# V turned by VectorE through HBM, and small TensorE tasks grouped, in the first stage of a hybrid decoder trunk

## The chip, the cores and the metric

The kernel runs on one core of a Trainium2 chip. The metric is device time in microseconds (us), from start to end of one execution. A core has five engines that run their own instruction lists side by side: TensorE (PE, matrix products, with its weight loads as PEld), VectorE (DVE), ScalarE (ACT), GpSimd (POOL) and SyncE (SP), which here issues nearly all transfers between HBM and the core's own memory (SBUF). TensorE writes its results into PSUM, from where DVE and ACT read them.

## The reference, cut to what matters

One layer: a norm, one input projection (2048 columns to 8 attention heads and 4 retention heads), both kinds of head, an output projection with a residual add, and a gated MLP with a short convolution. 16 meta tokens stand ahead of 256 tokens; the projections run over T = 272 tokens.

```python
proj = u @ w_in[l]
aq, ak, av, rq, rk, rv, rg = jnp.split(proj, SPLITS, axis=-1)
# diff_attention, per head: two softmaxes of 64 columns each, V of 128 columns
s = jnp.where(mask[None, None, None], s + bias[None, :, None], NEG_INF)
p = jax.nn.softmax(s, axis=-1)
a = (p[:, :, 0] - lam * p[:, :, 1]).astype(v.dtype)
return jnp.einsum('bhqk,bkhe->bqhe', a, v)
# retention, per head: scores times a decay table, V of 256 columns
s = jnp.einsum('bnihd,bnjhd->bnhij', q, k) * decay_in.astype(dt)[None, None]
intra = jnp.einsum('bnhij,bnjhe->bnihe', s, v)
...
ya = rmsnorm(ya, attn_subln[l]) * (1.0 - lam_init)
yr = rmsnorm(yr, ret_norm[l]) * jax.nn.silu(rg.reshape(B, L, R_HEADS, R_V_DIM))
y = jnp.concatenate([ya.reshape(B, L, D_A), yr.reshape(B, L, D_R)], axis=-1)
h = h + y @ w_out[l]
u = rmsnorm(h, ffn_norm[l]) * vmask
h = h + conv_glu(u, w_gate[l], w_up[l], conv_w[l], w_down[l])
```

Both kinds of head need V with the keys on the partitions, since the product of weights and values sums over keys. The kernel takes retention over the whole sequence at once, with decay tables in place of the chunks.

## The kernel before, in words

**The large products.** Features lie on the partitions, tokens in columns. A gemm makes one tile of 128 output features by 272 tokens (258, NQ, where the 14 leading ones are not needed) in PSUM, over 16 blocks (k-tiles) of 128 input features. Each block takes three products (L292 to L294): high part of the weight times high part of x, high times low, low times high, which together keep float32's precision. So a gemm is 48 matmuls. The weights of one gemm are one chunk of 1 MB (128 x 2048), loaded by SP (L95) into one of three `raw` buffers; ACT casts a half chunk into the high part `whi` (L107) and DVE subtracts to get the low part `wlo` (L108), three buffers each. Before each half gemm, `ahead` issues loads about two chunks forward and casts three halves forward.

**The first stage** takes the input projection. For each of 8 attention heads there are three gemms (q, k, v), for each of 4 retention heads four (k, q and two halves of v) and two more for its gates; the order of retention's parts is RSEQ: y0, g0, y1, g1, y2, y3, g2, g3. DVE multiplies each result with the norm's factor on its way out of PSUM (L546 for retention's v). Behind it come the output projection (16 gemms, L556 to L578, which also turns its results with DVE and stores them into an HBM scratch, `hd`, L573 and L576), 44 pairs of gate and up gemms, and the down projection.

**The heads' own work** is cut into small tasks, which wait in the list `side`; each gemm takes one task from it after every quarter (`pump`), so that they stand in TensorE's queue between the gemms' matmuls. All small matmuls and transposes are plain float32; a transpose is a matmul with the identity. An attention head has 12 tasks: the bias, three scores (softmax and difference, A), `vtr` (L371), three `atr` (L379), `av` (L391), `ytr` (L406) and two empty ones. `vtr` transposes V's three blocks of keys (100, 86 and 86 keys, KB) and copies them out of PSUM; `atr(i)` transposes the i + 1 blocks of A's row i; `av` makes the values and scales them; `ytr` transposes the head's result. A retention head has 10: three scores, three `vtr`, two `av` (one per half of V), `stats` (two products with ones, `rst`, and a reciprocal root) and `scale`; then two gate tasks. A program's names carry the head's number: `pv2` is the PSUM tile of V's transposes of attention head 2, `py` of the result's, `pa` of A's, `po` the values; `rv`, `rs` and `ro` are retention's V transposes, scores and values.

**The order.** The program is written gemm by gemm, but what each engine's list looks like in the end is set by a scheduler, which plays the program through with modelled durations when the kernel is built (`schedule_with_timeline_sim=True` in `build`) and appends what is ready. PSUM's eight banks bound it: three hold gemm results (`mm`), three are for small tasks (`misc`), two for scores of a head (`sc`, one buffer).

Of the kernel before, what the change touches and what calls it, by code (L numbers as in the profile page):

```python
# [10 lines left out]
F32 = mybir.dt.float32  # L11
# [4 lines left out]
ALU = mybir.AluOpType  # L16
# [3 lines left out]
P = 128  # L20
# [4 lines left out]
T = META + SEQ  # L25
Q0 = META - 2
NQ = T - Q0
QT = NQ // 3
TW = 288
XO = 32 - META  # L30
GO = 30
# [28 lines left out]
def trunk_kernel(ctx, tc, a, out):  # L60
# [91 lines left out]
    def misc(name):  # L152
        return ps1.tile([P, 512], F32, tag="misc", bufs=3, name=name)
# [145 lines left out]
    with ExitStack() as p1:  # L299
# [20 lines left out]

        nop = lambda: None

        def att_tasks(h, q, k, v):
            slope = 2.0 ** (-(h + 1))
# [45 lines left out]

            def vtr():  # L371
                ps = misc(f"pv{h}")
                for j, (b, e) in enumerate(KB):
                    PE.transpose(ps[:e - b, j * P:(j + 1) * P], v[:, b:e], idt)
                V.tensor_copy(out=vt[:KB[0][1], 0], in_=ps[:KB[0][1], :P])
                V.tensor_copy(out=vt[:QT, 1:3].rearrange("p a b -> p (a b)"),
                              in_=ps[:QT, P:3 * P])

            def atr(i):  # L379
                def f():  # L380
                    ps = misc(f"pa{h}_{i}")
                    for j in range(i + 1):
                        b, e = KB[j]
                        PE.transpose(ps[:e - b, j * P:j * P + QT], As[i][:, b:e], idt[:QT, :QT])
                    for j in range(i + 1):
                        b, e = KB[j]
                        (V.tensor_copy if j else S.copy)(
                            out=at[j][:e - b, i - j], in_=ps[:e - b, j * P:j * P + QT])
                return f

# [15 lines left out]
            def ytr():  # L406
                ps = misc(f"py{h}")
                for i in range(3):
# [9 lines left out]
        def ret_tasks(r, k, q, vs):  # L418
            dt_ = ap_.tile([P, 2, NQ], F32, tag="t", name=f"dk_{r}")
# [7 lines left out]

            def scores(j):
                def f():
                    b, e = KB[j]  # L430
                    n = (3 - j) * QT
                    ps = misc(f"rs{r}_{j}")
                    PE.matmul(ps[:e - b, :n], k[:, b:e], q[:, j * QT:], start=True, stop=True)
                    V.tensor_tensor(out=sd[j][:e - b], in0=ps[:e - b, :n], in1=dk[j],
                                    op=ALU.mult)
                return f

            def vtr(j):
                def f():
                    b, e = KB[j]  # L440
                    ps = misc(f"rv{r}_{j}")
                    for c in range(2):
                        PE.transpose(ps[:e - b, c * P:(c + 1) * P], vs[c][:, b:e], idt)
                    S.copy(out=vt[:e - b, j], in_=ps[:e - b, :2 * P])
                return f

            def av(c):
                def f():
                    if c == 0:
                        st["y"] = ps1.tile([P, 2, 512], F32, tag="sc", bufs=1, name=f"ro{r}")  # L450
                    y = st["y"]
                    cs = slice(c * P, (c + 1) * P)
                    for j, (b, e) in enumerate(KB):
                        n = e - b
                        o = y[:, c, j * QT:NQ]
                        PE.matmul(o, vt[:n, j, cs], sd[j][:n], start=(j == 0), stop=(j == 2))  # L456
# [3 lines left out]
                return f  # L460

# [14 lines left out]
            def scale():  # L476
                for c in range(2):
# [23 lines left out]
        for h in range(AH):  # L501
            q = ap_.tile([P, NQ], F32, tag="q", name=f"q{h}")
            k = ap_.tile([P, T], F32, tag="k", name=f"k{h}")
            v = ap_.tile([P, T], F32, tag="v", name=f"v{h}")
            ps = gemm(idx, xhi, xlo, Q0, NQ, 1)
            V.scalar_tensor_tensor(out=q, in0=ps[:, :NQ], scalar=0.125, in1=rq_,
                                   op0=ALU.mult, op1=ALU.mult)
            ps = gemm(idx + 1, xhi, xlo, 0, T, 1)
            V.tensor_tensor(out=k, in0=ps[:, :T], in1=rk_, op=ALU.mult)
            ps = gemm(idx + 2, xhi, xlo, 0, T, 1)  # L510
            V.tensor_tensor(out=v, in0=ps[:, :T], in1=rk_, op=ALU.mult)
            idx += 3
# [12 lines left out]
            side.extend(att_tasks(h, q2, (k2, kl), v))  # L525
        for kind, r in RSEQ:
            if kind == "g":
                for c in range(2):
                    g = ap_.tile([P, NQ], F32, tag=f"g{c}", name=f"rg{r}_{c}")
                    ps = gemm(idx, xhi, xlo, Q0, NQ, 1)  # L530
# [10 lines left out]
            V.tensor_tensor(out=q, in0=ps[:, :NQ], in1=rq_, op=ALU.mult)  # L541
            vs = []
            for c in range(2):
                v = ap_.tile([P, T], F32, tag="e" if c else "v", name=f"rv{r}_{c}")
                ps = gemm(idx + 2 + c, xhi, xlo, 0, T, 1)
                V.tensor_tensor(out=v, in0=ps[:, :T], in1=rk_, op=ALU.mult)  # L546
                vs.append(v)
            idx += 4
            side.extend(ret_tasks(r, k, q, vs))
        pump(len(side))  # L550
# [5 lines left out]
        for j in range(KT):  # L556
            xr = ap_.tile([P, NQ], F32, tag="g0", name=f"xres{j}")
            nc.sync.dma_start(out=xr, in_=a["x"][:, j, Q0:T])
            ps = gemm(idx + j, yhi, ylo, 0, NQ, 1)
            hT = ap_.tile([P, NQ], F32, tag="g1", name=f"hT{j}")  # L560
            V.tensor_tensor(out=hT, in0=ps[:, :NQ], in1=xr, op=ALU.add)
# [249 lines left out]
```

## Time and profile before

| | |
|---|---|
| median of the runs | 1181.98 us (1181.56 to 1183.25) |
| the profiled execution's own time | 1181.89 us |
| its span | 1180.1 us, granted TensorE clock 0.999 |
| TensorE busy | 1168.3 us, 99% of the span |
| first stage, 20 to 350 us | TensorE busy 329.2 of 330.0, DVE 253.8, ACT 177.8, DMA share 0.46 |
| output projection, 350 to 440 us | TensorE busy 89.1 of 90.0, DMA share 0.75 |
| gate and up gemms and what follows, 440 to 900 us | TensorE busy 460.0 of 460.0 |

The span runs from the first to the last instruction that the profiler saw; the execution's time is 1.8 us longer. A group's row shows line, engine, operation, written tile <- read tiles, partitions and shape, how many, then busy time, mean ns of one, and the idle time before them with what ended it. A row of the timeline shows start and duration in us. TensorE's matmuls overlap, so that their durations add up to more than the time they take. In rows for stretches of time the columns are the engines' busy times, the granted clock, the DMA share (mean busy share of 16 DMA engines) and GB/s.

### The profile page before, as it was taken

The page shows a single profiled execution, that of the slowest core. Times are in us where ns is not written, and L with a number is a line of the kernel's source. Part 1 is how long each engine was busy: PE and PEld are TensorE (multiplying, and loading weights), DVE is VectorE, ACT ScalarE, POOL GpSimd, SP SyncE. Part 2 cuts the span into 40 slices and gives each one's busy share as a digit, 9 for nine tenths or more (in the row PEclk, how much of TensorE's full clock was granted, in tenths as well). Part 3 has the DMA queues.
Part 4 walks back from the last instruction along what each step waited for, and adds up shares of the span by engine and source line. Part 5 has one row for each costly group of instructions (what it writes and reads, how often), then busy time and mean ns, then how long its engine had stood idle before and what let it go on. Part 6 is the DMA issues. An engine that isn't in the chain of part 4 may idle for free.

```text
span 1180.1 us, 19961 instructions
## 1 busy us (share of the span) xinstructions
PE 1168.3 (99%) x8087; PEld 1093.1 (93%) x8087; DVE 804.0 (68%) x1450; ACT 564.0 (48%) x887; POOL 2.0 (0%) x7
## 2 busy tenths in 40 slices
PE   9999999999999999999999999999999999999997
PEld 8999999999999999999999999999999888888886
DVE  7898877667677777776667776767767645454544
ACT  7566665544345444444444444444444434343442
POOL 0000000000000000000000000000000000000000
PEclk9999999999999999999999999999999999999999
DMA  8544344444448776555555555555555655555552
GB/s 308 189 154 160 144 144 157 167 166 146 151 156 262 227 226 230 184 192 195 180 179 182 188 195 185 179 180 190 191 190 179 214 207 186 194 198 183 194 194 106
DMA packets 53661, 219.82 MB, mean 186 GB/s; under 512 B 21763, under 2 KB 26091, under 8 KB 28609
## 3 DMA queue, kind: packets, MB, share of 16 engines
q1 hardware_dynamic: 53280, 217.36, 52.7%
q8 instruction: 63, 1.03, 0.3%
q0 software_dynamic: 144, 1.05, 0.2%
q14 instruction: 30, 0.24, 0.1%
q10 hardware_dynamic: 144, 0.14, 0.0%
HBM read 214.34 MB, written 4.19 MB: 185 GB/s over the span
## 4 chain that ended last, share of the span: by engine, by line
PE 97%; DMA 1%; DVE 1%; ACT 0%; issue 0%; SPq 0%; DVEq 0%; ACTq 0%
PE mm L292 17%; PE mm L293 17%; PE mm L294 17%; PE mm L288 14%; PE mm L290 7%; PE o L645 7%; PE o L646 7%; PE o L644 7%; PE po L396 1%; PE ro L456 1%; DMA raw<-in_w_first_dram 1%; PE mm L213 1%; PE mm L211 1%; PE mm L212 1%; PE mm L287 0%; PE sc L346 0%
## 5 line engine op out<-in xcount | busy, mean ns | idle before, releaser
L108 DVE TENSOR_TENSOR wlo<-raw,whi 128x1024 fp32r<-128x1024 f32 x381 | 466.1, 1224 | 245.8 <-ACT whi L107 240.7
L107 ACT CAST whi<-raw 128x1024 fp32r<-128x1024 f32 x381 | 400.3, 1051 | 472.6 <-PE mm L293 245.7
L288 PE MATMUL mm<-g,whi 128*128 128x512 f32 x704 | 249.1, 392 | 0.0
L292 PE MATMUL mm<-x,whi 128*128 128x272 f32 (+1 forms) x688 | 200.2, 291 | 0.0
L293 PE MATMUL mm<-g,whi 128*128 128x258 f32 x704 | 199.8, 284 | 0.0
L292 PE MATMUL mm<-g,whi 128*128 128x258 f32 x704 | 199.4, 283 | 0.0
L293 PE MATMUL mm<-x,whi 128*128 128x272 f32 (+1 forms) x688 | 199.2, 290 | 0.0
L294 PE MATMUL mm<-g,wlo 128*128 128x258 f32 x704 | 198.8, 282 | 0.0
L294 PE MATMUL mm<-x,wlo 128*128 128x272 f32 (+1 forms) x688 | 197.4, 287 | 0.8 <-DVE wlo L108 0.8
L290 PE MATMUL mm<-g,wlo 128*128 128x256 f32 x660 | 185.2, 281 | 0.0
L288 PEld LDWEIGHTS mm<-g,whi 128*128 128x128 f32 x704 | 132.1, 188 | 26.1
L293 PEld LDWEIGHTS mm<-g,whi 128*128 128x128 f32 x704 | 132.4, 188 | 1.9
L294 PEld LDWEIGHTS mm<-g,wlo 128*128 128x128 f32 x704 | 132.9, 189 | 0.0
L292 PEld LDWEIGHTS mm<-g,whi 128*128 128x128 f32 x704 | 132.4, 188 | 0.0
L294 PEld LDWEIGHTS mm<-x,wlo 128*128 128x128 f32 x688 | 129.6, 188 | 1.0 <-DVE wlo L108 1.0
L645 PE MATMUL o<-wlo,fhi 128*128 128x512 f32 x334 | 130.0, 389 | 0.0
L646 PE MATMUL o<-whi,flo 128*128 128x512 f32 x334 | 129.9, 389 | 0.0
L293 PEld LDWEIGHTS mm<-x,whi 128*128 128x128 f32 x688 | 129.7, 189 | 0.1
L292 PEld LDWEIGHTS mm<-x,whi 128*128 128x128 f32 x688 | 129.7, 188 | 0.1
L290 PEld LDWEIGHTS mm<-g,wlo 128*128 128x128 f32 x660 | 124.3, 188 | 0.0
L644 PE MATMUL o<-whi,fhi 128*128 128x512 f32 x334 | 117.0, 389 | 0.0
L644 PEld LDWEIGHTS o<-whi,fhi 128*128 128x128 f32 x334 | 62.7, 188 | 13.0
(245 smaller groups left out, 1376.3 us busy)
## 6 DMA issues: line engine op xcount, KB each, us to landing
raw<-in_w_in_dram SPq DMA_DIRECT2D x44, 1024.0 KB, 4.9
raw<-in_w_gate_dram SPq DMA_DIRECT2D x44, 1024.0 KB, 4.8
raw<-in_w_up_dram SPq DMA_DIRECT2D x44, 1024.0 KB, 4.8
raw<-in_w_down_dram SPq DMA_DIRECT2D x44, 1024.0 KB, 4.8
raw<-in_w_out_dram SPq DMA_DIRECT2D x16, 1024.0 KB, 5.0
raw<-in_w_first_dram SPq DMA_DIRECT2D x6, 512.0 KB, 7.6
xres<-in_x_dram SPq DMA_DIRECT2D x16, 129.0 KB, 4.5
hd<-hb SPq DMA_DIRECT2D x64, 32.0 KB, 3.7
```

What stands on the lines that cost most here:

```text
L107: S.copy(out=hi, in_=src)
L108: V.tensor_tensor(out=lo, in0=src, in1=hi.bitcast(F32), op=ALU.subtract)
L211: PE.matmul(o, wh, xh, start=(k == 0), stop=False)
L212: PE.matmul(o, wh, xl, start=False, stop=False)
L288: PE.matmul(ps[:, :2 * n], wh, xb, start=(k == 0), stop=(k == KT - 1))
L290: PE.matmul(ps[:, :n], wl, xh, start=False, stop=False)
L292: PE.matmul(ps[:, :n], wh, xh, start=(k == 0), stop=False)
L293: PE.matmul(ps[:, :n], wh, xl, start=False, stop=False)
L294: PE.matmul(ps[:, :n], wl, xh, start=False, stop=(k == KT - 1))
L644: PE.matmul(o, ah, wh, start=start and kk == 0, stop=False)
L645: PE.matmul(o, ah, wl, start=False, stop=False)
L646: PE.matmul(o, al, wh, start=False, stop=stop and kk == 1)
```

## The change

V is no longer transposed by TensorE. V's tile is 288 columns wide (TV, nine blocks of 32; POOL sets the last 16 columns to zero). In `turned`, DVE transposes it in blocks of 32 x 32 (one instruction of 128 x 288 per tile), and SP stores it in four parts into an HBM scratch, `hv`, in which rows are keys. A task then loads it into `vt` with the keys on the partitions by two transfers: one of the first 100 keys, one of the other two blocks of 86. For attention the load is the task `vload`, for retention `vtr`, which holds nothing else now.

The other small tasks are put together. A's six transposes are one task with two PSUM banks, and their copies, which were one per block, are one per block of keys (three per head). An attention head's result transposes no longer have their own task: they are put on a list, `late`, and done behind the values of the next head (the last one's behind retention head 0's values). Retention's three scores are one task and both halves of its values one. Empty tasks fill the lists, 12 and 10 long as before. The buffers of tags g0 and g1 grow to 288 columns; lines behind the change move by up to 15.

```diff
+        late = []
+        def turned(v, vb, hv, c):
+            V.transpose(out=vb, in_=v)
+            for i in range(4):
+                d = c * P + i * 32
+                nc.sync.dma_start(
+                    out=hv[:, d:d + 32].rearrange("(b t) f -> t b f", t=32),
+                    in_=vb[i * 32:(i + 1) * 32].rearrange("t (b f) -> t b f", f=32))
...
-            def vtr():
-                ps = misc(f"pv{h}")
+            def vload():
+                nc.sync.dma_start(out=vt[:KB[0][1], 0], in_=hv[:KB[0][1]])
+                nc.sync.dma_start(out=vt[:QT, 1:3],
+                                  in_=hv[KB[0][1]:T].rearrange("(a s) d -> s a d", s=QT))
+            def atr():
+                pa = [misc(f"pa{h}_0"), misc(f"pa{h}_1")]
                 for j, (b, e) in enumerate(KB):
-                    PE.transpose(ps[:e - b, j * P:(j + 1) * P], v[:, b:e], idt)
-                V.tensor_copy(out=vt[:KB[0][1], 0], in_=ps[:KB[0][1], :P])
-                V.tensor_copy(out=vt[:QT, 1:3].rearrange("p a b -> p (a b)"),
-                              in_=ps[:QT, P:3 * P])
...
+                    for i in range(j, 3):
+                        c = (i - j) * QT + (j == 1) * NQ
+                        PE.transpose(pa[j // 2][:e - b, c:c + QT], As[i][:, b:e],
+                                     idt[:QT, :QT])
...
-            return [prelude, scores(0), scores(1), vtr, scores(2), atr(0), atr(1), atr(2),
-                    nop, av, nop, ytr]
+            def values():
+                av()
+                while late:
+                    late.pop()()
+                late.append(ytr)
+            return [prelude, scores(0), scores(1), nop, scores(2), vload, nop, atr,
+                    nop, values, nop, nop]
...
-            def vtr(j):
-                def f():
-                    b, e = KB[j]
-                    ps = misc(f"rv{r}_{j}")
-                    for c in range(2):
-                        PE.transpose(ps[:e - b, c * P:(c + 1) * P], vs[c][:, b:e], idt)
-                    S.copy(out=vt[:e - b, j], in_=ps[:e - b, :2 * P])
-                return f
+            def vtr():
+                nc.sync.dma_start(out=vt[:KB[0][1], 0], in_=hv[:KB[0][1]])
+                nc.sync.dma_start(out=vt[:QT, 1:3],
+                                  in_=hv[KB[0][1]:T].rearrange("(a s) d -> s a d", s=QT))
...
-            return [scores(0), scores(1), scores(2), vtr(0), vtr(1), vtr(2), av(0), av(1),
-                    stats, scale]
+            return [scores, nop, vtr, nop, nop, av, nop, nop, stats, scale]
...
-            v = ap_.tile([P, T], F32, tag="v", name=f"v{h}")
+            v = ap_.tile([P, TV], F32, tag="v", name=f"v{h}")
+            nc.gpsimd.memset(v[:, T:], 0.0)
...
+            hv = dp.tile([TV, P], F32, name=f"hv{h}")
+            turned(v, ap_.tile([P, TV], F32, tag="g0", name=f"vb{h}"), hv, 0)
...
+            vb = ap_.tile([P, 2, TV], F32, tag="k2", name=f"rvb{r}")
+            hv = dp.tile([TV, 2 * P], F32, name=f"rhv{r}")
             for c in range(2):
-                v = ap_.tile([P, T], F32, tag="e" if c else "v", name=f"rv{r}_{c}")
+                v = ap_.tile([P, TV], F32, tag="e" if c else "v", name=f"rv{r}_{c}")
+                nc.gpsimd.memset(v[:, T:], 0.0)
                 ps = gemm(idx + 2 + c, xhi, xlo, 0, T, 1)
-                V.tensor_tensor(out=v, in0=ps[:, :T], in1=rk_, op=ALU.mult)
-                vs.append(v)
+                V.tensor_tensor(out=v[:, :T], in0=ps[:, :T], in1=rk_, op=ALU.mult)
+                turned(v, vb[:, c], hv, c)
```

How the rows move is shown at three places. A row has the line, the operation, the written tile <- what it reads, and the shape; names end in running numbers, which differ between the two programs. First, TensorE in attention, before: a run of small tasks within a gemm, in which result transposes (`py1`) and V's transposes of the next head (`pv2`) stand mixed.

```order
L409 MATMUL py1_1145<-c_ident_444,yo_1_705 128x86
L374 MATMUL pv2_1248<-c_ident_444,v2_709 100x128
L374 MATMUL pv2_1248<-c_ident_444,v2_709 86x128
L409 MATMUL py1_1145<-c_ident_444,yo_1_705 128x86
L374 MATMUL pv2_1248<-c_ident_444,v2_709 86x128
L409 MATMUL py1_1145<-c_ident_444,yo_1_705 128x86
L384 MATMUL pa2_0_1300<-c_ident_444,A2_0_1196 100x86
```

And after, where the `pv` rows are gone and the result transposes stand among the next head's values (`po3`):

```order
L404 MATMUL po3_1717<-vt3_1331,at3_0_1332 86x128 x2
L417 MATMUL py2_1750<-c_ident_444,yo_2_1019 128x86
L404 MATMUL po3_1717<-vt3_1331,at3_1_1333 86x128
L404 MATMUL po3_1717<-vt3_1331,at3_0_1332 86x128
L404 MATMUL po3_1717<-vt3_1331,at3_1_1333 86x128
L404 MATMUL po3_1717<-vt3_1331,at3_2_1334 86x128
L417 MATMUL py2_1750<-c_ident_444,yo_2_1019 128x86 x2
```

V's transposes have left TensorE's list, and the run now ends on two result transposes (`py2`, 86 columns each). Second, SP's list at the end of the first stage, before: weight chunks alone.

```order
L95 DMA raw44_4058<-in_w_in_dram 128x2048
L95 DMA raw45_4147<-in_w_in_dram 128x2048
L95 DMA raw46_4215<-in_w_in_dram 128x2048
L95 DMA raw47_4290<-in_w_in_dram 128x2048
L95 DMA raw48_4371<-in_w_out_dram 128x2048
L95 DMA raw49_4467<-in_w_out_dram 128x2048
```

After, with the stores of both halves of the last retention head's V (`rvb3` to `rhv3`) and its two loads (`rvt3`) between them:

```order
L96 DMA raw46_4238<-in_w_in_dram 128x2048
L329 DMA rhv3_4066<-rvb3_4065 32x9x32 x4
L96 DMA raw47_4310<-in_w_in_dram 128x2048
L329 DMA rhv3_4066<-rvb3_4065 32x9x32 x4
L454 DMA rvt3_4235<-rhv3_4066 100x256
L455 DMA rvt3_4235<-rhv3_4066 86x2x256
L96 DMA raw48_4383<-in_w_out_dram 128x2048
L96 DMA raw49_4479<-in_w_out_dram 128x2048
```

The first weight chunk of the output projection, `raw48`, is issued behind the loads of V, which wait for all stores. Third, TensorE where the last retention head's statistics (`rst3`) stand, before: in the last gemm of the first stage, mm47.

```order
L294 MATMUL mm47_4466<-x0_71,wlo94_4374 128x258
L470 MATMUL rst3_4395<-rmh3_4391,onesr_77 128x258
L292 MATMUL mm47_4466<-x0_71,whi94_4373 128x258
L293 MATMUL mm47_4466<-x0_71,whi94_4373 128x258
L294 MATMUL mm47_4466<-x0_71,wlo94_4374 128x258
L471 MATMUL rst3_4395<-rml3_4392,onesr_77 128x258
```

After, in the gemm ahead of it, mm46:

```order
L294 MATMUL mm46_4382<-x0_71,whi92_4312 128x258
L481 MATMUL rst3_4407<-rmh3_4403,onesr_77 128x258
L295 MATMUL mm46_4382<-x0_71,wlo92_4313 128x258
L293 MATMUL mm46_4382<-x0_71,whi92_4312 128x258
L294 MATMUL mm46_4382<-x0_71,whi92_4312 128x258
L482 MATMUL rst3_4407<-rml3_4404,onesr_77 128x258
```

The statistics, and with them the last head's result that the output projection reads, stand one gemm earlier.

More of the change, by code (lines that the diff above doesn't have):

```diff
@@ L29 @@
 TW = 288
+TV = 288
 XO = 32 - META
@@ L426, in ret_tasks, with scores, av @@
             st = {}
[L428 to L436, printed above, removed]
-            def vtr(j):
-                def f():
-                    b, e = KB[j]
-                    ps = misc(f"rv{r}_{j}")
-                    for c in range(2):
-                        PE.transpose(ps[:e - b, c * P:(c + 1) * P], vs[c][:, b:e], idt)
-                    S.copy(out=vt[:e - b, j], in_=ps[:e - b, :2 * P])
[L445 to L451, printed above, removed]
+            def scores():
+                pr = [misc(f"rs{r}_0"), misc(f"rs{r}_1")]
+                for j, (b, e) in enumerate(KB):
+                    n, d = (3 - j) * QT, (j == 1) * NQ
+                    PE.matmul(pr[j // 2][:e - b, d:d + n], k[:, b:e], q[:, j * QT:],
+                              start=True, stop=True)
+                for j, (b, e) in enumerate(KB):
+                    n, d = (3 - j) * QT, (j == 1) * NQ
+                    V.tensor_tensor(out=sd[j][:e - b], in0=pr[j // 2][:e - b, d:d + n],
+                                    in1=dk[j], op=ALU.mult)
+            def vtr():
+                nc.sync.dma_start(out=vt[:KB[0][1], 0], in_=hv[:KB[0][1]])
+                nc.sync.dma_start(out=vt[:QT, 1:3],
+                                  in_=hv[KB[0][1]:T].rearrange("(a s) d -> s a d", s=QT))
+            def av():
+                y = st["y"] = ps1.tile([P, 2, 512], F32, tag="sc", bufs=1, name=f"ro{r}")
+                for c in range(2):
                     cs = slice(c * P, (c + 1) * P)
@@ L454, in f @@
                         n = e - b
-                        o = y[:, c, j * QT:NQ]
-                        PE.matmul(o, vt[:n, j, cs], sd[j][:n], start=(j == 0), stop=(j == 2))
+                        PE.matmul(y[:, c, j * QT:NQ], vt[:n, j, cs], sd[j][:n],
+                                  start=(j == 0), stop=(j == 2))
+                for c in range(2):
                     q_ = ap_.tile([P, NQ], F32, tag="A", bufs=3, name=f"rsq{r}_{c}")
@@ L459, in f @@
                     st[c] = q_
-                return f
+                while late:
+                    late.pop()()
             def stats():
@@ L524, in trunk_kernel @@
                                 op=ALU.subtract)
-            side.extend(att_tasks(h, q2, (k2, kl), v))
+            side.extend(att_tasks(h, q2, (k2, kl), hv))
         for kind, r in RSEQ:
@@ L556, in trunk_kernel @@
         for j in range(KT):
[L557 removed]
+            xr = ap_.tile([P, TV], F32, tag="g0", name=f"xres{j}")[:, :NQ]
             nc.sync.dma_start(out=xr, in_=a["x"][:, j, Q0:T])
             ps = gemm(idx + j, yhi, ylo, 0, NQ, 1)
[L560 removed]
+            hT = ap_.tile([P, TV], F32, tag="g1", name=f"hT{j}")[:, :NQ]
             V.tensor_tensor(out=hT, in0=ps[:, :NQ], in1=xr, op=ALU.add)
```

24 lines of the change are left out of this document (10 added, 14 removed).

## The prediction

> **What bounds the kernel now.** I read the page's busy times and chain first, then the groups of TensorE by form, then the timeline around small tasks, and last the waits and the DMA of the stage that the change touches.
>
> ```profile
> span 1180.1 us, 19961 instructions
> PE 1168.3 (99%) x8087; PEld 1093.1 (93%) x8087; DVE 804.0 (68%) x1450; ACT 564.0 (48%) x887; POOL 2.0 (0%) x7
> PE 97%; DMA 1%; DVE 1%; ACT 0%; issue 0%; SPq 0%; DVEq 0%; ACTq 0%
> ACT whi L107 <- PE mm L293: 245.7, 168, 4.4
> ```
>
> TensorE is busy 99% of the span and 97% of the chain. The last row says that ScalarE, which casts the weights, waits 245.7 us for TensorE to give a cast buffer back: weights arrive ahead of their use, and TensorE sets the pace. So a change pays only by what it takes from TensorE's queue, and costs whatever makes that queue wait. In the windows (us, busy of PE, PEld, DVE, ACT, POOL, then clock, DMA share, GB/s) the stage that changes is full, and its end has a hole:
>
> ```profile
> 20.00:350.00 330.00, 329.23 (x2708) 328.05 (x2707) 253.84 (x668) 177.82 (x383) 1.09 (x2) 1.00 0.46 162
> 350.00:354.00 4.00, 3.09 (x22) 2.46 (x21) 3.23 (x6) 3.35 (x5) 0.00 (x0) 1.00 0.36 85
> ```
>
> **What a small task costs TensorE.** The groups give a transpose of V 272 ns, but matmuls overlap, so the price is the distance from start to start in the timeline.
>
> ```profile
> L443 PE MATMUL rv<-c_ident,rv 128*86 128x128 f32 x16 | 3.0, 272 | 0.0
> ...
> 61.14 0.29 PE L292 MATMUL mm<-x,whi 128*128 128x272 f32 x1
> 61.27 0.24 PE L384 MATMUL pa<-c_ident,A 86*100 86x86 f32 x1
> 61.30 0.37 PE L293 MATMUL mm<-x,whi 128*128 128x272 f32 x1
> 61.50 0.28 PE L294 MATMUL mm<-x,wlo 128*128 128x272 f32 x1
> 61.62 0.29 PE L292 MATMUL mm<-x,whi 128*128 128x272 f32 x1
> ...
> 92.16 0.27 PE L374 MATMUL pv<-c_ident,v 128*100 128x128 f32 x1
> 92.27 0.24 PE L409 MATMUL py<-c_ident,yo 86*128 86x86 f32 x1
> 92.35 0.38 PE L374 MATMUL pv<-c_ident,v 128*86 128x128 f32 x2
> 92.57 0.24 PE L409 MATMUL py<-c_ident,yo 86*128 86x86 f32 x1
> ...
> 242.12 0.89 PE L456 MATMUL ro<-sd,rvt 100*128 100x258 f32 x4
> 242.73 0.40 PE L294 MATMUL mm<-x,wlo 128*128 128x258 f32 x1
> ```
>
> Inside a run of small fp32 tasks a 128-column transpose takes 0.11 (92.16 to 92.27; two from 92.35 to 92.57) and an 86-column one 0.08. At a run's end (61.27) the next gemm matmul starts 0.03 later and its successor 0.20 after that, where 0.12 is usual: the last task costs 0.03 and the return 0.08, together 0.11, whatever its size. So a 128-column task costs the same inside a run or alone; an 86-column one is 0.03 cheaper inside; a wide fp32 product is dearer inside: the four passes from 242.12 (two of 258, two of 172 columns) take 0.61, which is 0.22 + 0.22 + 0.15 and 0.03 for the last.
>
> By that, the sum on TensorE. Removed: 24 transposes of V for attention and 24 for retention, 48 x 0.11 = 5.3 us. Grouping: in the two built orders the fp32 runs fall from 78 to 53, but what counts is the kind of task that stands last. Of the 25 ends that vanish, most were 128-column transposes, which gains nothing. Ends on an 86-column transpose rise from 32 to 41: nine of them dearer by 0.03, 0.3 lost. Ends on a wide pass fall from 10 to 3: seven passes that cost 0.11 now cost 0.15 or 0.22 inside their run, which over the two widths is 0.3 lost. Grouping costs 0.6. **Net -4.7 us.** Bounds: -5.3 without that loss, -4.1 with twice it.
>
> **DVE and ScalarE.** A transpose of 128x256 on DVE is a row of the output projection; the others are what goes.
>
> ```profile
> L573 DVE STREAM_TRANSPOSE hb<-hT 128x256 f32<-128x256 f32 x16 | 7.0, 442 | 0.4
> L546 DVE TENSOR_TENSOR rv<-mm,rstd 128x272 f32<-128x272 f32 x8 | 3.5, 438 | 2.6 <-PE mm L294 2.6
> L376 DVE COPY vt<-pv 86x256 f32<-86x256 f32 x8 | 3.3, 410 | 0.0
> L375 DVE COPY vt<-pv 100x128 f32<-100x128 f32 x8 | 2.3, 287 | 1.2 <-PE pv L374 1.1
> 53.02 0.29 PE L293 MATMUL mm<-x,whi 128*128 128x272 f32 x1
> 54.08 0.39 PE L294 MATMUL mm<-x,wlo 128*128 128x272 f32 x1 [0.78 <-DVE wlo L108]
> ```
>
> Added: 16 x 0.442 x 288/256 = 8.0 us on DVE; gone: 5.6 of copies, and A's copies merge 24 into 16. DVE stays near 254 of 330 us, under TensorE's cover, except where it is already late: at 53.02 TensorE waits 0.94 beyond its pace for DVE's wlo, and two of the new transposes (0.5 each) go into DVE's queue just there. Between 0 and 1.0; I take **+0.5**. The 16 memsets on POOL write 16 columns each, with POOL 0% busy; if they were late, the transposes behind them would be, by less than a memset.
>
> **The end of the stage.** TensorE's hole is where the last retention head's tail holds weight buffers:
>
> ```profile
> 351.17 0.28 PE L294 MATMUL mm<-yhi,wlo 128*128 128x258 f32 x1
> 351.75 0.39 PE L292 MATMUL mm<-yhi,whi 128*128 128x258 f32 x1 [0.30 <-ACT whi L107]
> 351.97 0.28 PE L293 MATMUL mm<-ylo,whi 128*128 128x258 f32 x1
> 352.70 0.39 PE L292 MATMUL mm<-yhi,whi 128*128 128x258 f32 x1 [0.44 <-ACT whi L107]
> 352.92 0.28 PE L293 MATMUL mm<-ylo,whi 128*128 128x258 f32 x1
> 353.37 0.39 PE L294 MATMUL mm<-yhi,wlo 128*128 128x258 f32 x1 [0.16 <-DVE wlo L108]
> ```
>
> Against 0.12 a step, the three cost 0.46 + 0.61 + 0.33 = 1.4. In the changed order the last head's statistics (rst3) stand a gemm of 48 matmuls, 5.8 us, earlier, so its last two k-tiles are ready before buffers run out. **-1.4**, bounds -1.4 and 0 (the hole stays).
>
> **The new wait.** V now goes multiply, transpose, four stores to HBM, then two loads, and the loads wait on SP for the stores to land; queued behind them on SP is the next weight load. The second load has 86 partitions. The rows that show such a load are the decay tables (100 partitions at 258.57, 86 at 258.92, 258 columns of f32), with nothing else in flight until the weights of 261.67 arrive; stores of this kind are hd's.
>
> ```profile
> 258.57 0.30 SPq L420 DMA_DIRECT2D dk<-in_decay_dram  x1
> 258.92 0.27 SPq L421 DMA_DIRECT2D dk<-in_decay_dram  x1
> 261.67 0.35 SPq L95 DMA_DIRECT2D raw<-in_w_in_dram  x1
> 260.80:261.30 0.50, 1.00 0.13 45
> 261.30:261.80 0.50, 1.00 0.12 41
> 261.80:262.30 0.50, 1.00 0.14 47
> 262.30:262.60 0.30, 1.00 0.06 21
> ...
> 352.08 3.93 SPq L576 DMA_DIRECT2D hd<-hb  x8
> DMA to landing us min/median/max: 1.6/3.8/7.3
> ```
>
> From 260.8 on the DMA share is 0.13 at some 44 GB/s: two of the sixteen engines carry the 86-partition table, and it is done 3.7 us after its issue, 2.0 for its 89 KB and 1.7 around them. Retention's second load has 86 x 2 x 1 KB = 176 KB: 4.0 + 1.7 = 5.7 us (estimate from these rows). The chain after the last gemm matmul of a head's second V half starts: 0.29 for it, 0.44 multiply, 0.50 transpose, 0.1 of hand-overs; the fourth store is issued 3 x 0.49 later, lands after 1.6 (alone) to 3.8 (median, behind weights), the 86-partition load is issued 0.5 after that and lands 5.7 later: 10.6 to 12.8 us. In the built order 76 rows stand between that matmul and the first value product of heads 1 and 2, 78 for head 3: 73 gemm steps at 0.122 and the scores' six passes, 0.92, make 9.8, and the first value product gives 0.4 more: the load is wanted at 10.2. Head 0 has 101 rows, 3 us more, and is covered; attention's loads are wanted some 250 rows (over 30 us) later, covered. So each of three heads waits 0.4 to 2.6; with the stores landing at 2.6 it is 1.4, in all 4.2. Head 1's load also queues behind head 3's tables on the same two engines (0 to 2.0, I take 0.4), and head 3's transpose stands behind a 1.2 us wlo in DVE's order (0 to 1.2, 0.6). **+5.2**, bounds 0 and 11.
>
> The weight load behind loses time on SP: some 2 to 4 us until the stores have landed, and on two engines it stands behind the 4.0 of rvt.
>
> ```profile
> raw<-in_w_in_dram SPq DMA_DIRECT2D x44, 1024.0 KB, 4.9
> ```
>
> A chunk of 1 MB feeds 48 matmuls, 5.9 us, and three such buffers and three cast ones (half a chunk each) stand between the queue and TensorE: a load is issued about two chunks, 11 to 12 us, ahead of its first matmul and needs 4.9 and two casts of 1.1, so some 5 are to spare, and the cast buffers hold 8.8 more that the 245.7 shows filled. I cost it at nothing; without that cover it would be 1 to 3 us at each head, the same sort of wait as (b) below.
>
> **Sum.** -4.7 + 0.5 - 1.4 + 5.2 = -0.4 us. The profiled execution took 1181.89 (1.8 around its span of 1180.1), the median is 1181.98, so the two can be exchanged here; I predict 1181.6. What TensorE saves, it waits away at three places.
>
> **Rivals.** (a) The loads land in time, because the second is spread over more engines or started sooner: -4.7 + 0.5 - 1.4 = -5.6, 1176.4. For it: nothing in the trace has this load itself, with two blocks per partition. Against it: the 0.13. [...] (b) Slower: the stores of heads 1 to 3 land behind a weight load at the median 3.8 or later, each head waits 2.6, and the two extras come to 2.2: 10.0 in all, net +4.4, 1186.4. It makes the kernel slower by more than 0.2% from waits of 8.0 together on. For it: weights are issued 2 to 3 us ahead of these stores; against it: the last of four stores waits less than the first. (c) Leaving the run is dear in itself, so that 25 fewer runs save another 25 x 0.08 = 2.0: 1179.6. Against it, 92.16 to 92.27 inside equals 0.11 at an end. (d) A transpose costs its 272 ns: 48 x 0.16 more saved, 7.7, 1173.9. [...]
>
> **How the numbers follow.** Forecast 0.46, with waits of 3.5 to 7.5 in all: 1179.9 to 1183.9; a change under 0.2% (2.4 us) can't be told from none. (a) 0.27, since the heart of the sum is a load that no row shows as it will be; (b) 0.21, (c) 0.04, (d) 0.02. Faster: (a), (c), (d) and 0.02 of the forecast's edge, 0.35; slower: (b) and 0.02 for the loss that twice the grouping's price would bring, 0.23; same 0.42. The range goes from 1175.5, which is (a) without grouping's loss and with half the crowding at 53, to 1186.9, which is (b) with all of it, and leaves out (d) and the farther tails of (a) and (b), under 0.2.
>
> **What would show it.** The transposes of V gone from TensorE, 48 fewer; TensorE idle before ro (retention's values) with rvt's load named, at three heads, 1 to 2.5 us each; no hole where the output projection begins; between 260 and 320 stretches with a DMA share near 0.13. Without waits before ro, (a) holds; with waits at all four heads or over 8 us, (b).

## The result

| | median us | range | ratio to before, 95% interval |
|---|---|---|---|
| before | 1181.77 | 1181.39 to 1183.25 | |
| changed | 1196.45 | 1194.08 to 1197.18 | 1.0117 [1.0106, 1.0129] |

The change makes the kernel slower, by 14.7 us. The forecast was 1181.6 with a range up to 1186.9, so both are missed. The page of the changed kernel (span, busy times, the chain by engine):

```profile
span 1195.1 us, 19983 instructions
PE 1172.1 (98%) x8039; PEld 1096.2 (92%) x8039; DVE 803.9 (67%) x1442; ACT 558.4 (47%) x859; POOL 3.7 (0%) x23
PE 91%; DMA 6%; DVE 2%; SPq 1%; issue 0%; ACT 0%; DVEq 0%; ACTq 0%
```

TensorE issues 48 fewer matmuls than before (8087 then) and is yet 3.8 us longer busy; the chain has 6% DMA where it had 1%. Two things are to be explained, then: time in which TensorE waits, and time in which it works more slowly. The waits of TensorE (in all, times, longest), and the timeline where retention's values (`ro`) start at the four heads; the bracket gives the idle time before a row and its releaser:

```profile
PE ro L464 <- DMA rvt<-rhv: 12.1, 4, 4.9
PE mm L295 <- DVE wlo L109: 0.9, 1, 0.9
```

```profile
214.47 1.67 PE L464 MATMUL ro<-sd,rvt 86*128 86x172 f32 x10 [0.82 <-DMA rvt<-rhv]
256.00 3.13 PE L464 MATMUL ro<-sd,rvt 86*128 86x172 f32 x10 [3.99 <-DMA rvt<-rhv]
302.79 3.13 PE L464 MATMUL ro<-sd,rvt 86*128 86x172 f32 x10 [4.86 <-DMA rvt<-rhv]
336.30 1.86 PE L464 MATMUL ro<-sd,rvt 86*128 86x172 f32 x10 [2.40 <-DMA rvt<-rhv]
```

At all four heads TensorE waits for the load of the 86-row blocks, 12.1 us in all. The same ten passes then take 1.67 at the first head and 3.13 at the two with the longest waits. The windows say why (the columns are those of the windows in the prediction; the third number from the end is the granted clock):

```profile
220.00:270.00 50.00, 46.01 (x345) 45.33 (x344) 29.72 (x52) 16.30 (x21) 0.22 (x2) 0.93 0.45 143
270.00:320.00 50.00, 45.14 (x333) 44.47 (x332) 29.02 (x49) 15.29 (x18) 0.00 (x0) 0.90 0.49 155
320.00:360.00 40.00, 37.60 (x293) 37.17 (x292) 27.37 (x50) 15.22 (x22) 0.00 (x0) 0.96 0.50 161
350.00:354.00 4.00, 4.00 (x36) 4.00 (x35) 3.57 (x8) 1.55 (x2) 0.00 (x0) 1.00 0.43 158
255.60:255.80 0.20, 0.00 (x0) 0.00 (x0) 0.00 (x0) 0.00 (x0) 0.00 (x0) 0.93 0.55 205
256.00:259.00 3.00, 3.00 (x11) 2.81 (x12) 0.00 (x0) 0.00 (x0) 0.00 (x0) 0.50 0.75 311
262.40:262.70 0.30, 0.30 (x4) 0.30 (x3) 0.00 (x0) 0.00 (x0) 0.00 (x0) 0.67 0.00 0
300.00:300.20 0.20, 0.00 (x0) 0.00 (x0) 0.00 (x0) 0.00 (x0) 0.00 (x0) 0.86 0.23 61
310.20:310.50 0.30, 0.30 (x4) 0.30 (x4) 0.00 (x0) 0.00 (x0) 0.00 (x0) 0.69 0.00 0
337.60:337.80 0.20, 0.20 (x4) 0.20 (x2) 0.00 (x0) 0.00 (x0) 0.00 (x0) 0.72 0.87 369
341.00:341.20 0.20, 0.20 (x3) 0.20 (x2) 0.00 (x0) 0.00 (x0) 0.00 (x0) 0.74 0.07 26
```

Before, the clock was 1.00 here throughout. Now it is 0.50 in three stretches, and each begins at a wait. A mean of 0.93 over 0.2 us, when the clock is 1.00 or 0.50 in every window of 0.25 us around these stretches that holds no edge, puts the start at 255.77; the other edges follow in the same way: 255.77 to 262.60 (6.83 us), 300.14 to 310.39 (10.25), 337.69 to 341.10 (3.41). Without the parts in which TensorE is still idle, it works 17.6 us at half clock and loses 8.8 by it. So 12.1 + 8.8 = 20.9 us are lost, against the 5.6 that rival (a) of the prediction gains: +15.3. The two spans differ by 15.0.

The hole at the end of the stage is gone, as foreseen (350 to 354: full). The chain of waits gives the durations of the transfers in question, from issue to landing: the last store of V where it was on the chain (`rhv`), and the load of the 86-row blocks (`rvt`).

```profile
202.70 4.21 DMA rhv<-rvb
207.39 6.94 DMA rvt<-rhv
244.38 2.71 DMA rhv<-rvb
247.50 8.36 DMA rvt<-rhv
294.71 7.95 DMA rvt<-rhv
327.12 1.70 DMA rhv<-rvb
329.38 6.88 DMA rvt<-rhv
```

The load was estimated at 5.7 and takes 6.9 to 8.4.

### The profile page after: what moved, and what is told of

It is laid out like the page before. It is cut to its first block, busy times and chain, and to the rows that moved or that the text cites. A ratio compares the mean times of both kernels' runs of the same rounds, so it can differ in the third digit from the quotient of the medians.

```text
span 1195.1 us, 19983 instructions
## 1 busy us (share of the span) xinstructions
PE 1172.1 (98%) x8039; PEld 1096.2 (92%) x8039; DVE 803.9 (67%) x1442; ACT 558.4 (47%) x859; POOL 3.7 (0%) x23
## 4 chain that ended last, share of the span: by engine, by line
PE 91%; DMA 6%; DVE 2%; SPq 1%; issue 0%; ACT 0%; DVEq 0%; ACTq 0%
PE mm L293 16%; PE mm L294 16%; PE mm L295 16%; PE mm L289 14%; PE mm L291 7%; PE o L659 6%; PE o L660 6%; PE o L661 6%; DMA rvt<-rhv 3%; DMA raw<-in_w_first_dram 2%; PE ro L464 1%; PE po L404 1%; DMA rhv<-rvb 1%; DMA raw<-in_w_in_dram 1%; DVE wlo L109 1%; PE mm L288 0%
## 5 line engine op out<-in xcount | busy, mean ns | idle before, releaser
L295 PEld LDWEIGHTS mm<-x,wlo 128*128 128x128 f32 x688 | 132.1, 192 | 1.2 <-DVE wlo L109 1.2
L293 PEld LDWEIGHTS mm<-x,whi 128*128 128x128 f32 x688 | 132.5, 193 | 0.0
L294 PEld LDWEIGHTS mm<-x,whi 128*128 128x128 f32 x688 | 132.3, 192 | 0.0
L661 PEld LDWEIGHTS o<-whi,flo 128*128 128x128 f32 x334 | 62.7, 188 | 13.0
```

The source lines that it names most:

```text
L293: PE.matmul(ps[:, :n], wh, xh, start=(k == 0), stop=False)
L294: PE.matmul(ps[:, :n], wh, xl, start=False, stop=False)
L295: PE.matmul(ps[:, :n], wl, xh, start=False, stop=(k == KT - 1))
L661: PE.matmul(o, al, wh, start=False, stop=stop and kk == 1)
```

## The experiments

One theory, W, was set against rivals. It has two parts: the 12.1 us come from a load that goes over two of the sixteen DMA engines, and the 8.8 us from the clock, which is granted at half after such a wait. Rival S: the scratch itself is slow. Rival C: the clock drops for another reason than the waits. Theory N and rival H, on the load's size, come with the run that tests them. Medians of before in these comparisons: 1181.75 to 1182.07.

**The load cut by partitions.** Nothing but the load of retention's V differs.

```diff
-nc.sync.dma_start(out=vt[:QT, 1:3], in_=hv[...].rearrange("(a s) d -> s a d", s=QT))
+hs = hv[KB[0][1]:T].rearrange("(a s) d -> s a d", s=QT)
+nc.sync.dma_start(out=vt[:80, 1:3], in_=hs[:80])
+nc.sync.dma_start(out=vt[80:QT, 1:3], in_=hs[80:])
```

> Retention's second load of V is cut by partitions, 80 and 6 instead of 86; TensorE's order is row for row that of the change. Theory W (two engines): the change loses 12.1 us in waits before ro since an 86-partition load goes over two of the sixteen DMA engines, and some 8.7 us more since TensorE's clock is granted at half for 3 to 7 us after a wait of 2 us and more. With 80 partitions on sixteen engines the load lands 4 to 5.5 us sooner than the 6.9 to 8.4 us of the change, waits before ro fall from 12.1 to under 1, the clock stays at 1.00 from 220 to 360 us, and the time is 1176 to 1178. Rival S (the scratch itself: stores, weights in the queue, write before read): the load lands little sooner, 8 us or more of the waits stay, 1189 to 1196.

Measured: 1176.78 us (1175.43 to 1178.38), ratio 0.9959 [0.9944, 0.9974]: faster than before. From its chain the only piece of `rvt` that is on it, and two windows:

```profile
287.72 2.62 DMA rvt<-rhv
220.00:270.00 50.00, 50.00 (x404) 49.77 (x403) 36.30 (x65) 19.65 (x24) 0.22 (x2) 1.00 0.52 171
270.00:320.00 50.00, 49.86 (x394) 49.08 (x394) 32.94 (x54) 18.23 (x24) 0.00 (x0) 1.00 0.57 184
```

The load lands 2.6 us after the last of its two issues and 3.0 after the first, instead of 8; TensorE is full but for 0.14 us, and the clock stays at 1.00. One line of the change holds its whole loss: 19.7 us between the medians. Rival S falls. The DMA share shows the difference as well. It was 0.13, two of sixteen engines, under the 86-partition table, and is 0.13 and 0.14 under the 86-row load alone (in the run without the weight chunk, below). Here, at head 3, the three pieces of V are issued from 313.10 to 313.79 and a weight chunk at 314.25. What moves from 313.75 to 315.50, some 288 KB by the rates of those windows, is about the 279 KB of the three pieces (272 rows of 1 KB), so the chunk has hardly begun in these two:

```profile
314.50:314.75 0.25, 0.25 (x5) 0.25 (x4) 0.02 (x1) 0.25 (x1) 0.00 (x0) 1.00 0.88 275
314.75:315.00 0.25, 0.25 (x5) 0.25 (x4) 0.00 (x0) 0.25 (x2) 0.00 (x0) 1.00 0.91 320
```

A share of 0.88 and 0.91 is some fourteen engines of sixteen, at 275 and 320 GB/s, with the first 100 keys among what they move. So the runs show that 86 rows go over two engines and the same rows as 80 and 6 over many; why, they do not show.

**The values later.**

```diff
-return [scores, nop, vtr, nop, nop, av, nop, nop, stats, scale]
+return [scores, nop, vtr] + [nop] * 6 + [av, nop, nop, stats, scale]
```

> Retention's values stand four tasks later in the list (48 rows of TensorE's order, 5.9 us at 0.122 a step), the load is as slow as in the change. Theory W: 5.9 us is more than the longest wait of 4.9, so no wait before ro is left and no half clock, though rvt's second load still takes 6.5 to 8.5 us; the last head's statistics stand a gemm later, so the hole of 1.4 at the stage's end may be back: 1176 to 1178.5. Rival C (the clock drops for another reason than TensorE's waits, as the work on DMA or DVE): granted clock still at 0.9 to 0.96 between 220 and 360 us, 1183 to 1188.

Measured: 1177.2 us (1177.02 to 1177.84), ratio 0.9963 [0.9949, 0.9977]. No wait before `ro` and a clock of 1.00 in every window, with the slow load still in place. So the loss can be taken away from the other side too, and neither the scratch nor the two-engine load lowers the clock by itself: rival C falls. The hole is back where the output projection begins, smaller than before:

```profile
348.06 0.39 PE L293 MATMUL mm<-yhi,whi 128*128 128x258 f32 x1 [0.43 <-ACT whi L108]
348.72 0.39 PE L295 MATMUL mm<-yhi,wlo 128*128 128x258 f32 x1 [0.16 <-DVE wlo L109]
```

**The wait filled with work.**

```diff
 y = st["y"] = ps1.tile([P, 2, 512], F32, tag="sc", bufs=1, name=f"ro{r}")
+for _ in range((0, 34, 40, 16)[r]):
+    PE.transpose(y[:, 0, 384:512], idt, idt)
```

> The change, with 34, 40 and 16 transposes of the identity (0.11 each, into unused columns of ro's banks) ahead of the values of retention heads 1, 2 and 3, where TensorE otherwise waits 4.1, 4.9 and 2.3 us. The load comes no sooner, so the 12.1 us from the load stay. Theory W: the half clock comes from the idling alone, so it stays away: the time falls by the 8.7 us that it costs, to 1186.5 to 1189. Rival C: the clock drops all the same, 1195 to 1198.

Measured: 1190.12 us (1188.37 to 1192.95), ratio 1.0073 [1.0057, 1.0090]. Its timeline at heads 1 and 2 and its waits and windows:

```profile
251.34 3.87 PE L461 MATMUL ro<-c_ident 128*128 128x128 f32 x34
293.69 4.53 PE L461 MATMUL ro<-c_ident 128*128 128x128 f32 x40
PE ro L466 <- DMA rvt<-rhv: 2.5, 2, 1.5
220.00:270.00 50.00, 50.00 (x408) 49.69 (x407) 33.09 (x58) 18.14 (x22) 0.22 (x2) 1.00 0.49 165
270.00:320.00 50.00, 50.00 (x405) 49.66 (x404) 31.52 (x54) 16.57 (x20) 0.00 (x0) 1.00 0.53 165
```

The useless work makes the kernel faster than the change: the load comes no sooner, 2.5 us of waits and 90 x 0.11 = 9.9 of filling stand where 12.1 of waits stood, but in the profiled execution the clock is not lowered in the first stage. Span against span the change loses 8.5 us more (1195.1 and 1186.6), which is the 8.8 worked out above. By medians it is 6.3, below what was expected, and this kernel's times scatter over 4.6 us. The profiled execution is the fastest of the four. The granted clock over a whole execution was recorded for all: 0.998 in the two faster ones (1188.37, 1189.20), as in kernels without such waits, but 0.996 and 0.995 in the two slower (1191.04, 1192.95). By that the slower ones lost some 2.4 and 3.6 us to half clock (an estimate, 0.002 and 0.003 of 1190), which is most of the scatter: the filling, with up to 1.51 us of wait left, did not keep the clock up every time.

**Half of the slow load.** The middle block of keys goes over 86 partitions as in the change, the last one as 80 and 6.

> As the change, but of retention's second load only the middle block of keys goes over 86 partitions (88 KB); the last block goes as 80 and 6 partitions ahead of it. Theory W: the slow load takes 2.0 us less on its two engines and is issued 0.7 later, so the waits before ro fall by some 1.3 each (in heads 1 and 3 the first products of the values also stand 4 to 6 rows sooner than the last): 0, 2.5 to 3, 3.5, 0.5, in all 6 to 7. Each wait of over 2 us brings a stretch of half clock of one or two times 3.3 us, 1.7 to 3.4 us lost each: 1186 to 1190. If the half clock came only with waits of 4 us and more, 1183 to 1184.

Measured: 1183.86 us (1181.72 to 1186.39), ratio 1.0015 [1.0006, 1.0024]. It lies below the 1186 to 1190 that theory W gave, because the waits are shorter than expected, 4.9 us in all:

```profile
252.99 2.48 PE L466 MATMUL ro<-sd,rvt 86*128 86x172 f32 x10 [1.57 <-DMA rvt<-rhv]
296.20 1.67 PE L466 MATMUL ro<-sd,rvt 86*128 86x172 f32 x10 [3.07 <-DMA rvt<-rhv]
253.70:253.90 0.20, 0.20 (x2) 0.12 (x1) 0.00 (x0) 0.00 (x0) 0.00 (x0) 0.59 0.10 41
298.00:298.20 0.20, 0.20 (x4) 0.20 (x3) 0.00 (x0) 0.20 (x2) 0.00 (x0) 0.78 0.96 410
```

The time alone would fit the reading that only waits of 4 us lower the clock (1183 to 1184); the profile contradicts it. Both waits, 1.57 and 3.07, bring a stretch of half clock, from 253.74 and from 298.11, each 3.41 long, which costs 1.7 apiece. The 1176.4 of rival (a), 4.9 of waits and 3.4 for the clock make 1184.7; the profiled execution took 1184.65.

**The same kernel once more**, for a second profile.

> The kernel with half of the slow load once more, unchanged, for a second profile. In its first profile waits of 1.57 and 3.07 us each brought one stretch of half clock, while in other kernels waits of 1.51 and 2.37 brought none. If a free-running window decides (how a wait falls across it), waits of 1.5 to 2.5 bring a stretch in one execution and not in another, and stretches stay multiples of 3.4 us; if the length of the wait decides, the same waits bring the same stretches.

Measured: 1185.53 us, with nearly the same waits:

```profile
252.63 1.70 PE L467 MATMUL ro<-sd,rvt 86*128 86x172 f32 x10 [1.53 <-DMA rvt<-rhv]
295.43 3.13 PE L467 MATMUL ro<-sd,rvt 86*128 86x172 f32 x10 [2.79 <-DMA rvt<-rhv]
254.30:254.50 0.20, 0.20 (x4) 0.20 (x3) 0.00 (x0) 0.14 (x1) 0.00 (x0) 0.74 0.57 205
295.30:295.50 0.20, 0.07 (x1) 0.10 (x1) 0.00 (x0) 0.00 (x0) 0.00 (x0) 0.64 1.81 287
```

The stretches begin at 254.40 and 295.36 and last 3.41 and, though the second wait is shorter than in the first profile, 6.83. So the length of the wait does not decide alone. The starts lie, within one execution, whole multiples of 3.413 us apart, 13.00 and 24.00 of them in the change (255.77, 300.14, 337.69), 13.00 in the first profile of this kernel, 12.00 in the second. They fit a grid of windows of 3.413 us, and the reading taken here is that what counts is how a wait falls across that grid. The window ahead of a stretch was not always idle throughout: the wait of 2.40 at head 3 of the change covered 2.0 us of the window that ends at 337.69, the waits of 1.57 and 1.53 here cannot have covered more than their length, and all three were followed by half clock. A wait of 1.51 (in the run with filled waits) and one of 2.37 (in the next run, quoted there) brought none.

Counted by window, the cases fall in order. Where the grid lies in an execution is known from any stretch on it, and each of the twelve profiles has one at its end, when TensorE has nothing left to do (in the change from 1191.02, 274 periods behind the first). Two examples, the next run's wait of 2.37 and that of 1.57 in this kernel's first profile. Each has two rows, the window that the wait lay in (of two, the later one) and the window behind it; TensorE's busy time is the second number:

```profile
252.34:255.75 3.41, 2.05 (x15) 2.03 (x16) 0.82 (x1) 0.35 (x2) 0.00 (x0) 1.00 0.45 132
255.75:259.17 3.42, 3.42 (x31) 3.42 (x30) 1.28 (x3) 1.64 (x4) 0.00 (x0) 1.00 0.45 187
250.32:253.74 3.42, 1.85 (x13) 1.58 (x12) 1.23 (x1) 1.05 (x1) 0.00 (x0) 1.00 0.63 193
253.74:257.15 3.41, 3.41 (x15) 3.23 (x15) 0.47 (x2) 1.07 (x3) 0.00 (x0) 0.50 0.94 317
```

The wait of 2.37 was split into 1.01 and 1.36 idle and brought nothing; that of 1.57 lay in one window and brought half clock. From 20 to 440 us of all profiles, twelve windows have 0.8 to 1.41 us idle and none was followed by half clock; twelve have 1.50 to 3.41 and eleven were. The exception is the first of two neighbours with 1.57 and 1.50, at head 2 of this kernel's first profile. After 2.65 idle or more, two windows ran at half clock, after 2.64 or less one; the change's stretch of three is one after 2.21 and two after 2.65. Eleven cases are few for a rule, and what exactly the chip counts stays open.

**Without the weight chunk behind the load.** Is the load itself slow, or what shares its engines? Four chunks of 1 MB, those issued right behind `rvt`, are left out, and four gemms compute with zeros.

```diff
+if c in (32, 38, 44, 48):
+    nc.gpsimd.memset(t, 0.0)
+    return
 nc.sync.dma_start(out=t, in_=chunks[c])
```

> The change without the weight chunk that is issued right behind rvt's loads (four chunks of 1 MB, 32, 38, 44 and 48, are left out: POOL fills the buffers with zeros, so four gemms compute zeros). TensorE's order is that of the change. Theory N (the two engines also carry their part of the weight chunk, 64 KB each, 2.6 us): rvt's second load lands 5.7 us after its issue at heads 2 and 3 (4.0 for 176 KB on two engines and 1.7 around it), 1.2 to 2.2 sooner than the 7.95 and 6.9 of the change; the waits before ro shrink by as much. At heads 0 and 1 decay tables stand on the same two engines, and less is gained. Rival H (the load itself is slow, since it reads scratch just written, or for its shape): it takes 7 to 8 us as before.

Measured: 1187.47 us in one execution. The load in the chain of waits; from the timeline the wait at head 1, whose ten passes run at full clock (1.67); all waits of the values; and two windows at head 2, between the issue of the two loads and SP's next issue at 294.39:

```profile
207.38 6.25 DMA rvt<-rhv
246.89 6.67 DMA rvt<-rhv
289.70 6.11 DMA rvt<-rhv
320.60 6.13 DMA rvt<-rhv
253.70 1.67 PE L467 MATMUL ro<-sd,rvt 86*128 86x172 f32 x10 [2.37 <-DMA rvt<-rhv]
PE ro L467 <- DMA rvt<-rhv: 7.7, 4, 3.4
292.00:293.00 1.00, 0.58 (x4) 0.17 (x2) 0.00 (x0) 0.94 (x1) 0.00 (x0) 1.00 0.13 47
293.00:294.00 1.00, 0.00 (x0) 0.00 (x0) 0.86 (x1) 0.11 (x1) 0.00 (x0) 1.00 0.14 49
```

With the chunk the load took 6.94, 8.36, 7.95 and 6.88. So the load costs 6.1 by itself, 0.4 above the estimate, and the chunk adds 0.7 to 1.8. Theory N holds, with the estimate a little low. The two windows show the load itself on two of the sixteen engines: a share of 0.13 to 0.14, at 47 to 49 GB/s. The waits are still 7.7 us in all, and waits of 3.36 and 1.63 bring one stretch of half clock each: 1176.4 of rival (a), 7.7 and 3.4 make 1187.5.

**Parts of the change.** Retention's V alone goes back to TensorE:

```diff
-turned(v, vb[:, c], hv, c)
+hv.append(v)
...
-return [scores, nop, vtr, nop, nop, av, nop, nop, stats, scale]
+return [scores, vtr(0), vtr(1), vtr(2), nop, av, nop, nop, stats, scale]
```

> Only retention's V goes back to TensorE's 24 transposes and ScalarE's copies; attention's V still goes through DVE and HBM, and the groups stay. Theory W: no waits, no half clock; against the change freed of waits 24 x 0.11 = 2.6 dearer: 1178 to 1180.5, and attention's 24 loads of V show no wait. Rival: attention's part or the grouping loses time by itself: above 1182.

Measured: 1178.38 us (1177.87 to 1180.35), ratio 0.9974 [0.9962, 0.9986], as expected: attention's loads have more than 250 rows before they are wanted, and none is waited for, although they have the same 86 partitions. Next, V of both kinds on TensorE, and only the grouping kept (`vload` and `vtr` hold the transposes of before):

> The grouping alone: V of attention and of retention is transposed by TensorE as before, A's transposes, values with the last result's transposes, retention's scores and values are grouped as in the change. The runs of small fp32 tasks fall from 78 to 69; priced by what stands last in a run, they cost 0.3 us more than before; the last head's statistics stand a gemm earlier than before, so the hole of 1.4 at the stage's end goes. Expected: 1180.3 to 1181.5, against 1181.87 of before. Rival (leaving a run is dear by itself): 9 x 0.08 = 0.7 less, 1179.6. Rival (grouped tasks wait longer for their inputs or for PSUM banks): idle before pa, po, rs or ro, above 1182.

Measured: 1180.89 us (1180.31 to 1182.91), ratio 0.9990 [0.9981, 0.9999], within what was expected. The last of these, V through HBM with the cut load and every task single as before:

> V through DVE and HBM for both kinds of head, retention's second load cut into 80 and 6 partitions, and no grouping: A's transposes, the result's transposes, scores and values are single tasks as before. Priced by the same rule the small tasks cost 0.4 us less than with the groups, and nothing waits: 1175.5 to 1177.5, the same as with the groups (1176.78) within what can be told. If the groups were worth what 14 fewer runs at 0.08 would give, it would be 1.1 slower: 1178.

Measured: 1176.45 us (1175.35 to 1180.49), ratio 0.9948 [0.9934, 0.9961], not to be told from the grouped one (1176.78). Fourteen more runs of small tasks cost nothing that these times, which scatter over 5.1 us, can show. The profiled execution is the slowest of the five. No value waits in it for its load; TensorE's longest wait in the stage is one for DVE, in attention, and half clock follows in the next window:

```profile
57.29 0.39 PE L295 MATMUL mm<-x,wlo 128*128 128x272 f32 x1 [2.19 <-DVE wlo L109]
58.65:62.06 3.41, 3.41 (x19) 3.41 (x18) 1.37 (x3) 0.70 (x1) 0.00 (x0) 0.50 0.93 326
```

So half clock followed idling of TensorE here too, where the wait, 2.19 us, was not for a transfer.

**Cut and a little later.** The cut load, and the values two tasks later.

> The load cut into 80 and 6 partitions (as in the run of that cut alone, 1176.78) and retention's values two tasks (some 24 rows, 2.9 us) later. The cut alone left a wait of some 0.2 at head 2 and times between 1175.4 and 1178.4. Theory W: with 2.9 us more no wait is left even when stores land late: 1175.5 to 1177, with less scatter; the last head's statistics are still in mm46, so the hole at the stage's end stays away. Rival: later values push the last head's tail into the output projection, as in the run with four tasks later: 1177 to 1178.

Measured: 1176.16 us (1175.58 to 1176.45), ratio 0.9952 [0.9938, 0.9965]. It beats both kernels, by 20.3 us the changed one and by 5.6 the one before, and scatters by 0.9 us where the cut alone scattered by 3.0.

## Why the prediction was wrong

**The step that failed is the new wait**, "+5.2, bounds 0 and 11". The place, the load and the two engines were right; the size was not, and a second price was missing.

Its first part, the wait itself, measured 12.1, above its own upper bound. The load was sized at 5.7 from the decay tables, which ran with nothing else in flight; in place it takes 6.9 to 8.4, together 7.3 over four heads beyond that size, and the waits are 6.9 beyond the forecast. In the one execution without the chunk behind the load the waits came to 7.7, so 4.4 of the 6.9 go with that chunk. The prediction asked what the load does to the weight chunk behind it on SP, found that covered (rightly: no row has TensorE waiting for `whi` in the changed kernel), and did not ask what the chunk does to the load on the two engines. Stores landed after 1.7 to 4.2, where 2.6 was taken and 3.8 was the upper bound. At head 0, held to be covered by 3 us, the last store came 1.6 later than taken and the load took 1.2 more: it waited 0.82, and still 0.3 without the chunk.

Its second part was not in the sum at all. The trace of before has TensorE's clock at 1.00 over the whole stage and no wait there above 0.8, so no row could price a wait of 4 us; the prediction then took a microsecond of waiting to cost a microsecond. The runs showed 8.8 us on top of 12.1, and the run with filled waits showed that they come from the idling. The prediction spoke of waits of 1 to 2.5 us, and rival (b) of 2.6; by the runs such waits can bring half clock, since 1.50 us idle in a window of 3.41 was enough once, and eleven of the twelve windows with that much or more were followed by it.

**The rest of the sum held.** Without waits it gave -5.6 (rival (a), 1176.4); the cut load gave 1176.78, the cut and later values 1176.16. In pieces: grouping and the hole, 0.3 by the same prices (69 runs) and -1.4, made -1.1 against a measured -1.2 (1182.07 to 1180.89). What is left for V by DVE, -5.6 + 1.1 = -4.5, stands against -4.1 (1180.89 to 1176.78). The crowding of DVE at 53 us was no sure part: TensorE's wait for `wlo` is 0.9 in the change and 1.5 in the kernel with grouping alone, which has no transpose of V on DVE, and 1.0 with the load cut; no row ties that wait to the transposes.

**The rivals.** (b) had the right sign and named waits before the values, but its path was late stores, and they were late at one of its three heads only (the last store took 2.71 at head 1 and 1.70 at head 3; at head 2 the load was issued 4.2 behind it). The rest of the excess came from the load, and with waits of 10.0 and no half clock it stopped at 1186.4. (a) was no account of this change and is nearly what the same change gives once its load is cut (1176.4 and 1176.78). (d) is out: 48 transposes were worth 4.1 and not 13 us. The runs speak against (c) without closing it: 14 runs of tasks more made no difference where 1.1 us was to be expected, but the scatter is larger than that, and grouping alone took 1180.89 where the same rival gave 1179.6 for it.

The profile would have shown, as the prediction named it, "waits at all four heads or over 8 us" for (b); both came.

## What to carry to other kernels

Price a wait on TensorE twice: its own length, and the half clock after it, which here followed eleven of the twelve 3.41 us windows with 1.50 us idle or more, and cost 1.7 us for each 3.41 us stretch and up to 3.8 us (7.6 us of work at half clock) for one wait of 4.9. Look at the partition count of every transfer that something waits for: 86 rows went over two engines (a DMA share of 0.13 to 0.14) and took 8.0 us where the same rows as 80 and 6 took 3.0, and the price of such a load in an idle moment was a lower bound: the chunk issued right behind it added 0.7 to 1.8 us. Moving work from the bound engine to memory pays only if the consumer is placed behind the landing with something to spare; here four tasks, 5.9 us, were enough for the slow load, and with the load cut two tasks, 2.9 us, left no wait and less scatter.

## What was not expected of the hardware

The half clock came in whole stretches of 3.41 us, one to three of them (3.41, 6.83, 10.25), on a grid that held over a whole execution (274 periods in the change); no window had to be idle throughout, 1.50 us of one was enough at head 2 of the first profile with half of the slow load. A wait of 3.07 brought one stretch in one execution, and one of 2.79 two in another. The changed kernel's times spread over 3.1 us, those of the version without waits over 0.9.
